# Moving half of a residual's gate rows behind a down projection, and five small loads to another DMA queue

## The chip, the core and the metric

The kernel runs on one core of a Trainium2 chip. The metric is the device time of one execution in microseconds; each time given is a median of several executions. In the profile PE is the matrix engine (TensorE), PEld its weight loads, DVE the vector engine, ACT the scalar engine, POOL GpSimd, and SP the engine whose queue issues most DMAs. An engine's name with a q behind it (ACTq, SPq) is its sequencer, which issues DMAs and waits.

## What is computed

A trunk of two layers over 512 tokens of width 1024, batch 1, in float32. Cut to what matters:

```python
for i in range(2):
    sh1, sc1, g1, sh2, sc2, g2 = split(silu(c) @ ada_w[i] + ada_b[i], 6)
    h = x * (1 + sc1) + sh1
    y = neighbourhood_mixer(h) if i == 0 else gqa_mixer(h)      # gqa: RMS-normed q, k with gains, rotary tables cos, sin
    x = layer_norm(ALPHA * x + (1 + g1) * y, ln_g[i, 0], ln_b[i, 0])
    h = x * (1 + sc2) + sh2
    y = hierarchical_moe(h)                                     # 32 experts, top 2: (silu(h Wg) * (h Wu)) Wd, weighted
    x = layer_norm(ALPHA * x + (1 + g2) * y, ln_g[i, 1], ln_b[i, 1])
```

The layer norm in front of the mixture leaves its gain and bias out at first; they are applied when x is needed again, as `x * ALPHA * ln_g + ALPHA * ln_b`. This is the step called `residual` below.

## The kernel before

Tokens lie in four tiles `X[0..3]` of 128 x 1024. Each layer is a mixer, its output projection and a router, and then the mixture of experts. Each expert takes up to 64 tokens, and two experts make a pair that fills 128 partitions. The 32 experts are 16 pairs, which the function `moe` goes through in 8 rounds `q` of two pairs, `a` and `b`. A round is, in the order of the code and of PE (whose order is written by hand here): `gate_up(a)` (products `gu` of the gathered tokens `xT` with 8 weight tiles of 1 MB), `turn` (four transposes), some filling work, `down(a)` (products `pd` of the transposed `hx` with 4 weight tiles of 1 MB), `gate_up(b)`, the gathering of the next round's tokens (products `gc` with the one-hot `OH`), and `down(b)`. In rounds 1 to 7 the filling work around `down(a)` adds the previous round's results to `X` (`combine`, also into tiles named `gc`).

In round 0 there is nothing to combine yet. There the filling work is `gate2` (the rows 1 + g2), `counts` (tokens per expert) and `residual(0)` and `residual(1)`, one for each half of 512 columns. Each of them spreads two rows of the modulation table over 128 partitions by a matmul, `pg` (gain) and `pb` (bias), into PSUM tiles named `gc`, of which there are two, and DVE then works through the four tiles of `X` with four pairs of instructions (lines 1367 and 1368):

```python
pg = pp.tile([P, F], F32, name="gc", bufs=2)
self.row(pg, l, 12 + h)
pb = pp.tile([P, F], F32, name="gc", bufs=2)
self.row(pb, l, 14 + h)
for t in range(NT):
    nc.vector.scalar_tensor_tensor(x, x, ALPHA, pg, op0=OP.mult, op1=OP.mult)
    nc.vector.scalar_tensor_tensor(x, pb, ALPHA, x, op0=OP.mult, op1=OP.add)
```

`self.row` is one matmul of 512 columns (two records in the trace). `down` writes the half x into `pd0` or `pd1`, and DVE (line 1413) and ACT (line 1414) and DVE again (line 1415) turn it into `YH` and `YL`.

All weights come through one queue, SP's, in a fixed order (`plan`), into a ring of buffers: the function `W` issues the next loads whenever buffers are free, and SP waits in its order for the PE instructions that read the buffer last. DVE, ACT and POOL are ordered by a scheduler.

`mixer1`, the second layer's mixer, begins with loads of the rotary tables (`rt`, from `in_rope`, one DMA) and of four rows of 64 norm weights (`gn`, tiles named `kk`, from `in_gain`, four DMAs, each spread over 128 partitions). POOL multiplies them (line 730) into the tables that the keys and queries use later. Beside that ACT and POOL or DVE split the first weights `w` (keys and values) into a high part `wh` (ACT, line 312) and a low part `wl` (line 313), PE transposes X into tiles `pt`, ACT makes `hTH` of it (line 419), and PE multiplies it with `wh` and `wl` into tiles `pj`.

Of the kernel before, what the change touches and what calls it, by code (L numbers as in the profile page):

```python
# [17 lines left out]
P = 128  # L18
# [5 lines left out]
HD = 64  # L24
# [37 lines left out]
def bcast(ap, shape):  # L62
    return ap.to_broadcast(shape)


class Trunk:
# [651 lines left out]
    def mixer1(self, st, qS):  # L718
        nc, a, tc = self.nc, self.a, self.tc
# [2 lines left out]
        V = qv.tile([P, NT, 256], F32, name="V")  # L722
        with tc.tile_pool(reuse_waits="tile", name="m1", bufs=1) as pool, tc.tile_pool(reuse_waits="tile", name="m1p", bufs=2, space=PSUM) as pp:
            rt = pool.tile([P, 4, NT, HD], F32, name="rt")
            nc.scalar.dma_start(rt[:, 0:2], a["rope"])
            gn = pool.tile([P, 4, HD], F32, name="kk", bufs=6)
            for i in range(4):
                nc.scalar.dma_start(gn[:, i, :], bcast(a["gain"][i:i + 1], [P, HD]))
            for i in (2, 3, 0, 1):
                nc.gpsimd.tensor_tensor(rt[:, i], rt[:, i % 2], bcast(gn[:, i:i + 1, :], [P, NT, HD]), op=OP.mult)  # L730
            hH = pool.tile([P, KD, S], F32R, name="hTH")
# [547 lines left out]
    def moe(self, l, zH, zL, G2, rt, OH):  # L1279
        nc, X, tc = self.nc, self.X, self.tc  # L1280
        NQ = E // 4
        with tc.tile_pool(reuse_waits="tile", name=f"mo{l}", bufs=2) as pool, \
# [35 lines left out]
            def gather(q, kk):  # L1318
                if kk == 0:
                    xT[q] = pool.tile([P, KD, 256], F32, name="xT", bufs=1)  # L1320
                ps = pp.tile([P, 2, 256], F32, name="gc", bufs=2)
                for k2 in range(2):
                    k = 2 * kk + k2
                    for t in range(NT):
                        for x, hh in ((0, zH), (1, zL)):
                            self.mm(ps[:, k2, :], hh[t][:, 128 * k:128 * k + 128], oh[:, t, :],
                                    t == 0 and x == 0, t == NT - 1 and x == 1)
                for k2 in range(2):
                    scaled(q, 2 * kk + k2, ps[:, k2, :])
# [20 lines left out]
            def combine(js, t, h):  # L1350
                c = slice(512 * h, 512 * h + 512)
                ps = pp.tile([P, F], F32, name="gc", bufs=2)
                n = 0
                for j in js:
                    for y in (YH, YL):
                        self.mm(ps, OT[j][:, t, :], y[j][:, c], n == 0, n == 2 * len(js) - 1)
                        n += 1
                nc.vector.tensor_tensor(X[t][:, c], X[t][:, c], ps, op=OP.add)  # L1358

            def residual(h):  # L1360
# [5 lines that stand above are left out]
                    x = X[t][:, 512 * h:512 * h + 512]  # L1366
                    nc.vector.scalar_tensor_tensor(x, x, ALPHA, pg, op0=OP.mult, op1=OP.mult)
                    nc.vector.scalar_tensor_tensor(x, pb, ALPHA, x, op0=OP.mult, op1=OP.add)

            def gate2(h):  # L1370
                ps = pp.tile([P, F], F32, name="tp", bufs=2)
                self.row(ps, l, 10 + h)
                nc.vector.tensor_scalar(G2[:, 512 * h:512 * h + 512], ps, 1.0, None, op0=OP.add)

            def gate_up(j):
                q, o = j // 2, 128 * (j % 2)
                gu = []
                for n in range(2):
                    g = pp.tile([P, F], F32, name=f"gu{n}")
                    gu.append(g)  # L1380
                    for kh in range(2):
                        w = [self.W(("gu", l, 2 * j + i, n, kh)).rearrange("p (k n) -> p k n", k=4) for i in range(2)]
                        for k in range(4):
                            kk = 4 * kh + k
                            for i in range(2):
                                self.mm(g[64 * i:64 * i + 64], xT[q][:, kk, o + 64 * i:o + 64 * i + 64], w[i][:, k, :],
                                        kk == 0, kk == KD - 1)
                    if n == 0:
                        h = pool.tile([P, F], F32, name="h", bufs=1)
                        nc.scalar.activation(h, gu[0], AF.Silu)  # L1390
                nc.vector.tensor_tensor(h, h, gu[1], op=OP.mult)  # L1391
                return h

            def turn(h):
                pt = pp.tile([P, 4, P], F32, name="tp", bufs=2)
                for f in range(4):
                    self.tr(pt[:, f, :], h[:, 128 * f:128 * f + 128])
                hx = pool.tile([P, F], F32, name="hx", bufs=1).rearrange("p (f s) -> p f s", f=4)
                nc.scalar.activation(hx, pt, AF.Copy)
                return hx  # L1400

            def down(j, hx):
                YH[j] = pool.tile([P, D], F32R, name="YH", bufs=2)
                YL[j] = pool.tile([P, D], F32R, name="YL", bufs=2)
                for x in range(2):
                    pd = pp.tile([P, F], F32, name=f"pd{x}")
                    w = [self.W(("dn", l, 2 * j + i, x)).rearrange("p (k n) -> p k n", k=4) for i in range(2)]
                    for f in range(4):
                        for i in range(2):
                            self.mm(pd[64 * i:64 * i + 64], hx[:, f, 64 * i:64 * i + 64], w[i][:, f, :], f == 0, f == 3)  # L1410
                    c = slice(512 * x, 512 * x + 512)
                    y = pool.tile([P, F], F32, name=("h", "hx")[x], bufs=1)
                    nc.vector.scalar_tensor_tensor(y, pd, GS[j][:, 2:3], G2[:, c], op0=OP.mult, op1=OP.mult)  # L1413
                    nc.scalar.activation(YH[j][:, c], y, AF.Copy)  # L1414
                    nc.vector.tensor_tensor(YL[j][:, c], y, YH[j][:, c].bitcast(F32), op=OP.subtract)
# [3 lines left out]
            def seed(ns):  # L1419
                for n in ns:  # L1420
                    h, t = units[n]
                    tag = ("gc", "gc", "gu0", "tp", "gu1", "tp", "pd0", "pd1")[n]
                    acc[h, t] = pp.tile([P, F], F32, name=tag, bufs=2 if n in (0, 1, 3, 5) else 1)
                    if n < NSEED[1]:
                        self.mm(acc[h, t], self.ident, X[t][:, 512 * h:512 * h + 512], True, False)
# [24 lines left out]
            for q in range(NQ):  # L1450
                a, b = 2 * q, 2 * q + 1
                h = gate_up(a)
                if q == 0:
                    fill = [lambda: gate2(0), lambda: gate2(1), lambda: self.counts(pool, pp, rt),
                            lambda: residual(0), lambda: residual(1)]
                else:
                    fill = [lambda t=t, x=x: combine((a - 2, a - 1), t, x) for t, x in th]
                for f in fill[:2]:
                    f()
                hx = turn(h)  # L1460
                for f in fill[2:]:
                    f()
                down(a, hx)
                if q + 1 < NQ:
                    self.mark(OH, rt, q + 1, 0, NT)
                else:
                    XR = [self.take() for _ in range(2)]
                    rt["XR"] = [XR[t // 2][:, D * (t % 2):D * (t % 2) + D] for t in range(NT)]
                h = gate_up(b)
                if q + 1 < NQ:  # L1470
                    gather(q + 1, 0)
                    hx = turn(h)
                    gather(q + 1, 1)
                    for n in range(2):
                        slots(a + 2, n)
                        gather(q + 1, 2 + n)
                    for n in range(2):
                        slots(b + 2, n)
                else:
                    self.act_table("natural_log_exp_and_others")  # L1480
                    for t, x in th[:2]:
                        combine((a,), t, x)
                    hx = turn(h)
                    for t, x in th[2:]:
                        combine((a,), t, x)
                    if l == DEPTH - 1:
                        rt["out"] = self.rows(l, pool.tile([P, KD, 256], F32, name="xT", bufs=1), pp, "gc", 2)
                    seed(range(NSEED[0]))
                down(b, hx)
# [146 lines left out]
```

## Time and profile before

| | |
|---|---|
| time, median of 3 executions | 1670.0 us (1669.55 to 1672.5) |
| the profiled execution | 1673.29 us, span of its instructions 1671.6 us |
| busy share of the span | PE 94%, PEld 54%, DVE 42%, ACT 26%, POOL 10% |
| mean granted PE clock | 0.972 of full speed |
| DMA | 493.17 MB, mean 295 GB/s |

The page cuts the span into 40 slices and tells for each how busy the engines were, which clock PE was granted and what the DMA engines moved. The timeline lists instructions in order of time, with the idle time before them and what ended it. The chain of waits is followed back from the last instruction. The windows give busy time by stretch.

### The profile page before, as it was taken

How to read it: one execution, taken by the hardware profiler on the slowest of the kernel's cores; microseconds unless marked ns; L12 is line 12 of the kernel's file. 1: busy time of each engine (PE TensorE's matmuls, PEld its weight loads, DVE VectorE, ACT ScalarE, POOL GpSimd, SP SyncE). 2: the span in 40 equal slices, each digit the busy share in tenths (PEclk: the TensorE clock that was granted, in tenths of full speed). 3: DMA queues.
4: the chain of work that ended last, by engine and by line, in shares of the span. 5: the costliest groups of instructions: out<-in, count | busy, mean ns of one | idle time of the engine just before them, and what ended most of it. 6: DMA issues, size and time to landing. Idle time of an engine off the chain costs nothing. (4 is left out here: it accounts for less than half of the span.)

```text
span 1671.6 us, 21362 instructions
## 1 busy us (share of the span) xinstructions
PE 1574.7 (94%) x8490; PEld 906.6 (54%) x8490; DVE 700.6 (42%) x1605; ACT 437.6 (26%) x934; POOL 162.3 (10%) x99
## 2 busy tenths in 40 slices
PE   7899997989999999999979989998999999999995
PEld 4676664773544545455448866766354545545442
DVE  3434545574232322323256865666432232323235
ACT  2343335231110111111134475453011111101112
POOL 2322212010000000000014250011000000000001
PEclk9999997999999999999989989999999999999997
DMA  9587872357999999999932000035899999999981
GB/s 328 196 309 269 331 306 104 137 202 295 417 419 420 419 419 420 419 419 420 420 125 102 26 1 25 1 125 206 368 416 420 420 420 420 419 420 420 419 332 51
DMA packets 76198, 493.17 MB, mean 295 GB/s; under 512 B 9876, under 2 KB 11284, under 8 KB 18876
## 3 DMA queue, kind: packets, MB, share of 16 engines
q1 hardware_dynamic: 71916, 485.05, 71.4%
q10 hardware_dynamic: 4176, 6.69, 1.2%
q8 instruction: 69, 1.13, 0.3%
q14 instruction: 37, 0.30, 0.1%
HBM read 489.61 MB, written 2.10 MB: 294 GB/s over the span
## 5 line engine op out<-in xcount | busy, mean ns | idle before, releaser
L300 PE MATMUL gu<-w,xT 128*64 128x512 f32 x2048 | 445.0, 592 | 0.0
L300 PEld LDWEIGHTS gu<-w,xT 128*64 128x64 f32 x2048 | 146.8, 137 | 291.6 <-issue 287.0
L300 PE MATMUL pd<-w,hx 128*64 128x512 f32 x1024 | 228.0, 598 | 0.0
L1391 DVE TENSOR_TENSOR h<-h,gu 128x512 f32<-128x512 f32 x32 | 22.0, 688 | 370.4 <-PE gu L300 370.4
L300 PEld LDWEIGHTS pd<-w,hx 128*64 128x64 f32 x1024 | 70.9, 137 | 140.3 <-issue 136.7
L300 PE MATMUL gc<-OH,zH 128*128 128x256 f32 x480 | 121.5, 291 | 2.6 <-DVE OH L1276 2.6
L300 PE MATMUL gc<-OH,zL 128*128 128x256 f32 x480 | 118.6, 284 | 0.0
L300 PE MATMUL gc<-YH,OT 128*128 128x512 f32 x244 | 104.2, 427 | 1.0 <-DVE X L1358 1.0
L1358 DVE TENSOR_TENSOR X<-X,gc 128x512 f32<-128x512 f32 x128 | 87.4, 688 | 39.3 <-PE gc L300 39.3
L300 PEld LDWEIGHTS gc<-OH,zH 128*128 128x128 f32 x480 | 92.5, 193 | 14.9 <-issue 11.4
L300 PE MATMUL gc<-YL,OT 128*128 128x512 f32 x244 | 96.3, 394 | 0.0
L300 PEld LDWEIGHTS gc<-OH,zL 128*128 128x128 f32 x480 | 92.6, 193 | 0.0
L300 PE MATMUL pw<-w,oH 128*128 128x512 f32 x256 | 86.3, 408 | 0.0
L1414 ACT ACTIVATE YH<-h 128x512 fp32r<-128x512 f32 x32 | 20.2, 630 | 233.6 <-DVE h L1413 233.6
L300 PE MATMUL pj<-wh,hTH 128*128 128x256 f32 (+1 forms) x272 | 71.2, 304 | 9.1 <-ACT hTH L419 4.0
L1294 ACT ACTIVATE xT<-gc,A 128x256 f32<-128x256 f32 x60 | 33.8, 566 | 173.9 <-PE gc L300 173.9
L300 PE MATMUL pj<-wl,hTH 128*128 128x256 f32 (+1 forms) x272 | 68.0, 292 | 0.0
L300 PE MATMUL pj<-wh,hTL 128*128 128x256 f32 (+1 forms) x272 | 65.6, 293 | 0.8 <-DVE hTL L427 0.8
L300 PEld LDWEIGHTS gc<-YH,OT 128*128 128x128 f32 x244 | 45.8, 188 | 37.3 <-DVE X L1358 15.8
L1292 DVE TENSOR_SCALAR xT<-gc,A 128x256 f32<-128x256 f32 x60 | 32.5, 545 | 76.9 <-ACT xT L1294 76.5
L1390 ACT ACTIVATE h<-gu 128x512 f32<-128x512 f32 x32 | 19.1, 597 | 173.0 <-PE gu L300 173.0
L303 PE MATMUL pt<-c_ident,pr 128*128 128x128 f32 x384 | 59.5, 283 | 2.1 <-ACT pr L862 2.0
(345 smaller groups left out, 2355.9 us busy)
## 6 DMA issues: line engine op xcount, KB each, us to landing
w<-in_gu SPq DMA_DIRECT2D x256, 1024.0 KB, 14.3
w<-in_dn SPq DMA_DIRECT2D x128, 1024.0 KB, 13.5
w<-in_ada SPq DMA_DIRECT2D x40, 1024.0 KB, 7.9
wq<-in_wqk SPq DMA_DIRECT2D x16, 512.0 KB, 3.6
w<-in_wo SPq DMA_DIRECT2D x8, 1024.0 KB, 5.8
w<-in_adaq SPq DMA_DIRECT2D x6, 1024.0 KB, 12.0
bias<-in_nab ACTq DMA_DIRECT2D x24, 256.0 KB, 3.4
w<-in_wq SPq DMA_DIRECT2D x4, 1024.0 KB, 4.9
```

Source lines behind the costliest of these rows:

```text
L300: return self.nc.tensor.matmul(out, l, r, start=start, stop=stop, **kw)
L303: self.nc.tensor.transpose(out, in_, self.ident)
L1292: nc.vector.tensor_scalar(xT[q][:, k, :], ps, s, b, op0=OP.mult, op1=OP.add)
L1294: nc.scalar.activation(xT[q][:, k, :], ps, AF.Identity, scale=s, bias=b)
L1358: nc.vector.tensor_tensor(X[t][:, c], X[t][:, c], ps, op=OP.add)
L1390: nc.scalar.activation(h, gu[0], AF.Silu)
L1391: nc.vector.tensor_tensor(h, h, gu[1], op=OP.mult)
L1414: nc.scalar.activation(YH[j][:, c], y, AF.Copy)
```

## The change

Two edits. In `moe`, round 0 no longer does `residual(1)` in front of `down(a)`, but right behind it. In `mixer1`, the five small loads are issued by SP's queue instead of ACT's.

```diff
@@ mixer1
             rt = pool.tile([P, 4, NT, HD], F32, name="rt")
-            nc.scalar.dma_start(rt[:, 0:2], a["rope"])
+            nc.sync.dma_start(rt[:, 0:2], a["rope"])
             gn = pool.tile([P, 4, HD], F32, name="kk", bufs=6)
             for i in range(4):
-                nc.scalar.dma_start(gn[:, i, :], bcast(a["gain"][i:i + 1], [P, HD]))
+                nc.sync.dma_start(gn[:, i, :], bcast(a["gain"][i:i + 1], [P, HD]))
@@ moe
                 if q == 0:
-                    fill = [lambda: gate2(0), lambda: gate2(1), lambda: self.counts(pool, pp, rt),
-                            lambda: residual(0), lambda: residual(1)]
+                    fill = [lambda: gate2(0), lambda: gate2(1), lambda: self.counts(pool, pp, rt), lambda: residual(0)]
                 else:
                     fill = [lambda t=t, x=x: combine((a - 2, a - 1), t, x) for t, x in th]
...
                 for f in fill[2:]:
                     f()
                 down(a, hx)
+                if q == 0:
+                    residual(1)
```

In the first layer, PE's rows between the counting product and `down(a)` were these (`mod` is the modulation table, `c_indc` picks a row of it):

```order
L300 LDWEIGHTS ones
L300 MATMUL tp<-Mb,ones 128x32
L300 MATMUL gc<-mod_67,c_indc 128x512 x4
L300 MATMUL pd_3298<-w_3178,hx 64x512
L300 MATMUL pd_3298<-w_3180,hx 64x512
```

Now two of the four row products stand there, and the end of `down(a)` with the start of `gate_up(b)` (`gu`) reads so:

```order
L300 MATMUL pd_3303<-w_3182,hx 64x512
L300 MATMUL pd_3303<-w_3184,hx 64x512
L300 MATMUL gc<-mod_67,c_indc 128x512 x2
L300 MATMUL gu_3333<-w_3186,xT 64x512
L300 MATMUL gu_3333<-w_3188,xT 64x512
```

The two products of `residual(1)` have moved behind the 16 of `down(a)`. The second layer has the same difference.

On DVE, in the first layer, behind the last instruction of `residual(0)` (the first row; X_63 to X_66 are the four tiles of X, L1158 to L1162 belong to `counts`):

```order
 L1368 SCALAR_TENSOR_TENSOR X_66<-gc,X_66 128x512
+L1413 SCALAR_TENSOR_TENSOR h<-pd_3286,GS,G_3009 128x512
+L1415 TENSOR_TENSOR YL<-h,YH 128x512
+L1158 TENSOR_SCALAR hx<-cntx 128x32 x7
+L1159 TENSOR_REDUCE nbx<-hx 128x32
 L1367 SCALAR_TENSOR_TENSOR X_63<-X_63,gc 128x512
+L1161 TENSOR_REDUCE hx<-nbx 128x1
 L1367 SCALAR_TENSOR_TENSOR X_64<-X_64,gc 128x512
+L1162 CAST tot<-hx 128x1
 L1368 SCALAR_TENSOR_TENSOR X_63<-gc,X_63 128x512
+L1413 SCALAR_TENSOR_TENSOR hx<-pd_3303,GS,G_3009 128x512
 L1368 SCALAR_TENSOR_TENSOR X_64<-gc,X_64 128x512
```

The first half of `down(a)` and the counts are now worked off ahead of the eight instructions of `residual(1)`, and the second half in the midst of them.

At the start of `mixer1`, ACT's rows (the first two are the end of the branch that closes the first layer):

```order
 L1169 UNCONDITIONAL_BRANCH x2
-L725 DMA rt<-in_rope 128x512
-L728 DMA kk<-in_gain 128x64 x4
 L312 ACTIVATE wh<-w_5752 128x1024 x2
 L419 ACTIVATE hTH<-pt,c_6307 128x512 x2
```

and SP's, where the loads now stand ahead of the fourth load of query weights:

```order
 L1169 UNCONDITIONAL_BRANCH x2
+L725 DMA rt<-in_rope 128x512
+L728 DMA kk<-in_gain 128x64 x4
 L272 DMA w_6311<-in_wq 128x2048
 L272 DMA w_6534<-in_wo 128x2048
```

ACT now goes from the branch straight to the split of the weights. PE's scheduler also puts two transposes of this stage some 25 products later than before.

## Rows read from the trace of the kernel before

**Rows 1.** Page: GB/s moved by DMA in 40 equal slices of the span.

```profile
GB/s 328 196 309 269 331 306 104 137 202 295 417 419 420 419 419 420 419 419 420 420 125 102 26 1 25 1 125 206 368 416 420 420 420 420 419 420 420 419 332 51
```

**Rows 2.** Timeline of PE, first layer, round 0: start, duration, instruction, idle before.

```profile
393.50 1.96 PE L300 MATMUL gc<-mod,c_indc 128*128 128x512 f32 x4
398.45 3.78 PE L300 MATMUL gc<-mod,c_indc 128*128 128x512 f32 x4 [2.99 <-DVE X L1367]
402.16 8.27 PE L300 MATMUL pd<-w,hx 128*64 128x512 f32 x32
410.27 13.90 PE L300 MATMUL gu<-w,xT 128*64 128x512 f32 x64
```

**Rows 3.** Timeline of DVE, same stretch.

```profile
394.72 1.28 DVE L1367 SCALAR_TENSOR_TENSOR X<-X,gc 128x512 f32<-128x512 f32 x2 [0.84 <-PE gc L300]
...
398.31 1.28 DVE L1368 SCALAR_TENSOR_TENSOR X<-gc,X 128x512 f32<-128x512 f32 x2
...
407.08 0.75 DVE L1413 SCALAR_TENSOR_TENSOR h<-pd,GS,G 128x512 f32<-128x512 f32 x1 [1.13 <-PE pd L300]
...
410.51 0.71 DVE L1158 TENSOR_SCALAR hx<-cntx 128x32 f32<-128x32 f32 x7 [1.29 <-PE pd L300]
```

**Rows 4.** Timeline of PE, second layer, round 0.

```profile
1181.13 1.96 PE L300 MATMUL gc<-mod,c_indc 128*128 128x512 f32 x4
1186.09 3.67 PE L300 MATMUL gc<-mod,c_indc 128*128 128x512 f32 x4 [2.99 <-DVE X L1367]
1189.68 7.09 PE L300 MATMUL pd<-w,hx 128*64 128x512 f32 x32
1196.60 13.90 PE L300 MATMUL gu<-w,xT 128*64 128x512 f32 x64
```

**Rows 5.** Chain of waits in order of time: start, duration, what.

```profile
906.17 0.86 PE pg L300 x2
...
1226.74 13.73 PE gu L300 x64
...
1285.77 13.73 PE gu L300 x64
```

**Rows 6.** Windows: busy time of each engine; last PEclk, DMA share, GB/s.

```profile
403.00:408.00 5.00, 5.00 (x22) 1.60 (x20) 3.70 (x6) 0.14 (x1) 0.00 (x0) 0.84 0.00 0
1191.00:1194.00 3.00, 3.00 (x16) 1.00 (x14) 3.00 (x6) 0.00 (x0) 0.00 (x0) 1.00 0.00 0
```

**Rows 7.** Timeline of SP, near the first layer's end.

```profile
807.16 0.33 SPq L272 DMA_DIRECT2D w<-in_gu  x1
```

**Rows 8.** DMA issues of 807 to 808 us: count, size, us to landing.

```profile
w<-in_gu SPq DMA_DIRECT2D x1, 1024.0 KB, 20.5
```

**Rows 9.** Timeline of PE, the first layer's last `gate_up`.

```profile
823.57 13.90 PE L300 MATMUL gu<-w,xT 128*64 128x512 f32 x64
```

**Rows 10.** Timeline of ACT at the start of `mixer1`.

```profile
867.88 0.34 ACTq L725 DMA_DIRECT2D rt<-in_rope  x1
868.33 1.81 ACTq L728 DMA_DIRECT2D kk<-in_gain  x4
870.19 2.00 ACT L312 ACTIVATE wh<-w 128x1024 fp32r<-128x1024 f32 x2 [2.48 <-DMA rt<-in_rope]
...
881.12 0.78 ACT L419 ACTIVATE hTH<-pt,c 128x512 fp32r<-128x512 f32 x1 [2.84 <-PE pt L303]
```

**Rows 11.** Timeline of PE at the start of `mixer1`.

```profile
867.85 1.94 PE L303 MATMUL pt<-c_ident,X 128*128 128x128 f32 x8 [6.23 <-ACTq L1169]
872.91 0.58 PE L300 MATMUL pj<-wh,hTH 128*128 128x256 f32 x1 [3.12 <-ACT hTH L419]
```

**Rows 12.** Windows of the same stage, as in rows 6.

```profile
875.00:879.00 4.00, 4.00 (x20) 4.00 (x20) 1.60 (x2) 2.54 (x4) 4.00 (x4) 0.50 0.10 16
879.00:885.00 6.00, 4.93 (x40) 4.46 (x39) 2.18 (x2) 3.88 (x6) 4.64 (x2) 1.00 0.58 183
```

**Rows 13.** Timeline of SP around the start of `mixer1`.

```profile
834.08 44.11 SPq L272 DMA_DIRECT2D w<-in_wq  x4
```

## The prediction

> **What bounds the kernel now.** I read the page first, then the windows, then the timelines of the three places that the change touches, PE and its partner engine side by side. PE is busy for 94% of the span, so a saving counts only where PE stands still or where PE's own work gets less, and only if the weights keep up.
>
> Two long stretches of the page, the expert stages of the two layers, move 416 to 420 GB/s all the time [rows 1]. The reader is to see two things running flat out together there. One round of two pairs takes PE 1285.77 - 1226.74 = 59.03 us [rows 5], and it eats 24 tiles of 1 MB (8 + 4 for each pair), 25.17 million bytes, which at 419.5 GB/s take 60.0 us. So the stream is a little slower than PE, loses about 1 us on it in each round, and lives on the lead that it has when the stage begins. What is left of the lead at the end decides whether PE may become faster. Near the first layer's end a tile was issued at 807.16 and landed 20.5 us later, at 827.7 [rows 7, 8]. It is one of the fourth pair of tiles of the gate_up that starts at 823.57 and lasts 13.90 [rows 9], so it is needed at 823.57 + 3/4 x 13.9 = 834.0. It lay there for 6.3 us. PE, not the stream, sets the pace up to the end.
>
> In round 0 the reader is to see PE standing still. The first half's row products start at 393.50, and the next ones only at 398.45, because both PSUM tiles are held until DVE has worked through X [rows 2, 3]. DVE takes 394.72 to 398.31 for three double rows, that is 0.60 us for each of its eight instructions. down follows only at 402.16. PE's clock has meanwhile fallen to its lower level (1.2 of 2.4 GHz; 0.84 of the full one over 403 to 408 [rows 6]), and the four products of the second half, which take 1.72 us at full clock (two records in 0.86 [rows 5]), take 3.7. The second layer shows the same [rows 4].
>
> At the start of mixer1, PE has 8 transposes from 867.85 on, and then waits 3.12 us for ACT [rows 11]. ACT issues five DMAs from 867.88 to 868.33 + 1.81 = 870.14, and its first split starts at 870.19 [rows 10]. The view puts that wait down to the landing of the rotary table. But the split reads neither table, and it starts 0.05 us behind the last issue: ACT was its own hindrance.
>
> **The change, part by part.** *residual(1) behind down, first layer.* Nothing of the arithmetic goes away. down can now start right behind the first half's products, at 393.50 + 1.72 = 395.22, since hx and the weights are long there. At full clock down takes 1196.60 - 1189.68 = 6.92 us [rows 4]. The moved products add 1.72. gate_up(b) starts at 395.22 + 6.92 + 1.72 = 403.86 instead of 410.27 [rows 2]: **6.4 us**. Of this, 1.2 us are the slow clock in down itself (410.27 - 402.16 - 6.92). If the clock fell all the same, 5.2 would be left; I take the whole, since PE's long idle time is gone.
>
> *Second layer.* By the same sum 1181.13 + 1.72 + 6.92 + 1.72 = 1191.49 instead of 1196.60 [rows 4]: **5.1 us**.
>
> What hides the eight DVE instructions: they ran in PE's way and now run beside gate_up(b), 13.73 us [rows 5]. At down's end, at 402.1, DVE is free (residual(0) is done at 399.6, the first evacuation at 0.75 + an ACT step + 0.75 some 2 us later [rows 3]). What it then has is 0.71 + three small reductions (under 0.75 together) + 8 x 0.60 + 2 x 0.75 = 7.8 us, and the next that PE needs of it is the product h, 1.72 + 13.73 = 15.4 us after down's end. There are 7 us to spare. The moved products' PSUM tiles are released by residual(0)'s reads at 399.6, 2.5 us before PE comes to them. Nothing else is late next on these engines.
>
> *Does the stream follow?* In both layers it stood with all buffers full, while PE stalled: no byte moves from 403 to 408 and from 1191 to 1194 [rows 6]. down frees those buffers 6.9 us earlier now, and the stream goes on without that gap. So it gains about what PE gains, at least 5 and 3 us. Even if it gained nothing in the first layer, a lead of 6.3 against 6.4 would lose 0.1 us.
>
> *Five DMAs on SP.* ACT saves their issue: its split can start at 867.88 instead of 870.19, **2.3 us** [rows 10]. PE's transposes end at 869.79, the two splits (2.00) at 869.9, so the whole chain of ACT, hTH and PE moves by the same 2.3. The loads cost SP as much, but SP's next load, the fourth of query weights, left only at the end of a row that lasts to 834.08 + 44.11 = 878.2, because its buffer is read until then [rows 13]; so SP has time. The places that the loads write were free by 867.88 at the latest, when ACT's first issue went out, so POOL's tables come no later than before either. Bounds: 0, if the row's reading is right and the landing was what ACT waited for, and 2.3. I take 2.3, as the 0.05 us speak for it. The rule of the Trainium skill (DMA: Bandwidth & Descriptors, section Issuing engines are not separate DMA queues) is that another issuing engine saves only the sequencer's time for starting a DMA, which is usually small beside the transfer. By "usually small" this term would be about 0 and the sum 11.5; the row says 2.3 us of ACT's own time, on the path, for five small DMAs.
>
> *Clock in mixer1.* PE runs at half clock (0.50, so 1.2 GHz) there until 879, and at the full one behind it [rows 12], so its 6.1 us of products from 872.91 on [rows 11] would be 3.0 us at full clock, and ACT waits 2.84 us for them at 881.12 [rows 10]. With the gap of 3.12 us behind the transposes shrunk to 0.8, the clock may rise earlier in PE's work: at most 3.0 us more. It may also rise later; I let that cost 1.5 us, half of the spread of the runs shown. Nearest is the row of before, so I take **0.5 us**.
>
> PE's two transposes that the scheduler moved cost nothing: PE does the same rows without a gap in that stretch (4.00 of 4.00 us busy [rows 12]).
>
> Sum: 6.4 + 5.1 + 2.3 + 0.5 = 14.3 us. The profiled execution took 1673.3 us, 3.3 above the median of 1670.0 and 1.7 above its span. All terms are differences inside it, so they are taken from the median: **1655.7 us**.
>
> **The rivals.** *The ACT edit does nothing on the path.* For it: the view's own releaser. Against it: the 0.05 us. Time: 1670.0 - 11.5 = 1658.5.
>
> *The stream takes the gain back.* If the weights set the pace of the expert stage, PE would wait for them before its end, and only the second edit would count: 1670.0 - 2.8 = 1667.2. For it: 60.0 us against 59.03 in each round. Against it: 6.3 us of lead at the end, and the gap in the stream that closes. The Trainium skill (DMA: Bandwidth & Descriptors, section Specifications) gives about 358 GB/s as one core's share of the HBM. By that the stream would be behind PE from the start and this rival would hold. The rows show 416 to 420 [rows 1].
>
> *Slower: the clock.* gate_up(b) now comes right behind the moved products. Should PE get only half clock in it, 13.73 us become 27.5 in each layer: 1670.0 - 14.3 + 27.5 = 1683. It decides from 28 us of additional half clock on. For it: the clock did fall just ahead of this place before [rows 6]. Against it: only after 3 us in which PE did nothing, and that idle time goes.
>
> **How the numbers follow.** The forecast 0.78, the ACT edit without effect 0.14, the stream 0.05, the clock 0.03. The forecast's own bounds are 1670.0 - 11.5 - 2.3 - 3.0 = 1653.2 and 1670.0 - (11.5 - 1.2) - 2.3 + 1.5 = 1658.9. With the first rival and the scatter of a median the range is 1653.0 to 1660.0. A measurement of this kernel tells about 0.2% (3.3 us) from no change. The first two cases are faster by more (0.92), the stream's 2.8 us count as the same (0.05), and the clock's case is slower (0.03).
>
> **What would show it.** Right: in both layers down starts some 1.8 us behind the first row products, PE has no wait on line 1367, the two moved products lie between pd and gu, and gate_up(b) starts 10.4 us behind the first row products (393.50 to 403.9). DVE has the second evacuation done before gate_up(b) ends, and DMA has no empty stretch in round 0. In mixer1, ACT's first split follows its last normalisation at once, and PE's wait behind the 8 transposes is under 1 us. Wrong: waits of PE on w<-in_gu or w<-in_dn late in a layer, a new wait of ACT's first split on another DMA, POOL's tables holding up the low parts of the weights, or half clock inside gate_up.

## The result and the profile after

The changed kernel took 1659.12 us (median of 5 executions, 1656.66 to 1660.54), beside it the kernel before 1671.91 (5 executions, 1669.55 to 1674.84). The ratio is 0.9925, with a 95% interval of 0.9910 to 0.9941: 12.5 us less, between 9.9 and 15.0. The profiled execution took 1659.12 us, its span is 1657.4 (1671.6 before).

The timeline of PE in the first layer's round 0 (start, duration, instruction) now reads:

```profile
393.49 1.96 PE L300 MATMUL gc<-mod,c_indc 128*128 128x512 f32 x4
395.38 7.09 PE L300 MATMUL pd<-w,hx 128*64 128x512 f32 x32
402.40 1.98 PE L300 MATMUL gc<-mod,c_indc 128*128 128x512 f32 x4
404.31 13.95 PE L300 MATMUL gu<-w,xT 128*64 128x512 f32 x64
```

Against [rows 2], the wait for line 1367 is gone, `down` runs at full clock, and `gate_up(b)` starts 10.82 us behind the first row product instead of 16.77. The second layer, same view, is the same to 0.01 us, where [rows 4] had 15.47:

```profile
1171.56 1.96 PE L300 MATMUL gc<-mod,c_indc 128*128 128x512 f32 x4
1173.45 7.09 PE L300 MATMUL pd<-w,hx 128*64 128x512 f32 x32
1180.47 1.98 PE L300 MATMUL gc<-mod,c_indc 128*128 128x512 f32 x4
1182.38 13.95 PE L300 MATMUL gu<-w,xT 128*64 128x512 f32 x64
```

DVE works off the first half of `down` at once, and the last of its eight moved instructions in the first layer is done at 410, 8 us before `gate_up(b)` ends at 418.2 (timeline of DVE):

```profile
399.50 0.74 DVE L1413 SCALAR_TENSOR_TENSOR h<-pd,GS,G 128x512 f32<-128x512 f32 x1
...
409.30 0.69 DVE L1368 SCALAR_TENSOR_TENSOR X<-gc,X 128x512 f32<-128x512 f32 x1
418.41 0.69 DVE L1391 TENSOR_TENSOR h<-h,gu 128x512 f32<-128x512 f32 x1 [8.41 <-PE gu L300]
```

The windows of both places (busy time of each engine; the last three columns are PE's clock, DMA share and GB/s) show the stream without its gap [rows 6], and PE at full clock:

```profile
403.00:408.00 5.00, 5.00 (x22) 1.66 (x22) 4.97 (x14) 0.63 (x1) 0.00 (x0) 1.00 1.01 418
1180.00:1192.00 12.00, 12.00 (x54) 4.02 (x52) 7.37 (x20) 1.23 (x2) 0.00 (x0) 1.00 1.02 422
```

At the start of `mixer1`, the timelines of SP, ACT and PE:

```profile
855.94 0.34 SPq L725 DMA_DIRECT2D rt<-in_rope  x1
861.95 1.75 SPq L728 DMA_DIRECT2D kk<-in_gain  x4
```

```profile
859.65 2.23 ACT L1542 ACTIVATE X<-w,rsx 128x512 f32<-128x512 f32 x3 [1.11 <-DVE rsx L1092]
862.04 2.00 ACT L312 ACTIVATE wh<-w 128x1024 fp32r<-128x1024 f32 x2 [0.17 <-ACTq L1169]
```

```profile
862.02 1.94 PE L303 MATMUL pt<-c_ident,X 128*128 128x128 f32 x8 [6.25 <-ACTq L1169]
864.77 0.58 PE L300 MATMUL pj<-wh,hTH 128*128 128x256 f32 x1 [0.81 <-ACT hTH L419]
```

ACT's split follows its last normalisation (done at 861.88) 0.16 us later, and PE waits 0.81 us behind its transposes instead of 3.12 [rows 11].

To see where all the time went I cut each profiled execution at PE instructions that every kernel has: the start of the first layer's first `gate_up` (front), from the end of a round-0 `gate_up(a)` to the start of `gate_up(b)` (round 0 of either layer), from there to the layer's last `gate_up` (experts), from the first of `mixer1`'s transposes to its first product `pj` (issue), from there to the last `pj`, and from the last `pj` to the second layer's first `gate_up` (rest of mixer). All values but the span are differences of starts in us. The stages left out agree to 0.4 us, apart from two: in e7 it is 45.13 us instead of some 44.3 from the last `gate_up` to the transposes, and in e1 and e2 the second layer's first `gate_up` takes 15.0 and 15.1 us instead of 13.9.

| kernel | front | round 0, first | experts, first | issue | pj | rest of mixer | round 0, second | span |
|---|---|---|---|---|---|---|---|---|
| before | 376.75 | 19.63 | 413.30 | 5.06 | 94.88 | 196.59 | 18.33 | 1671.6 |
| changed | 376.74 | 13.69 | 413.42 | 2.75 | 94.89 | 195.15 | 13.69 | 1657.4 |
| changed, again (e11) | 373.92 | 13.69 | 413.39 | 2.75 | 95.41 | 195.38 | 13.69 | 1655.4 |
| rows only (e1) | 371.95 | 13.69 | 413.41 | 5.07 | 94.96 | 194.35 | 13.69 | 1655.3 |
| rows only, again (e12) | 376.42 | 13.69 | 413.43 | 5.07 | 95.04 | 196.65 | 13.69 | 1661.1 |
| loads only (e2) | 372.96 | 16.99 | 413.37 | 2.75 | 95.41 | 196.07 | 18.34 | 1664.1 |
| table on ACT (e3) | 374.40 | 13.69 | 413.40 | 3.13 | 95.28 | 195.67 | 13.69 | 1656.3 |
| other PSUM (e4) | 375.66 | 13.39 | 413.34 | 2.75 | 95.34 | 195.19 | 13.39 | 1656.1 |
| both behind (e5) | 374.86 | 20.96 | 413.85 | 2.75 | 94.70 | 195.14 | 20.96 | 1670.5 |
| two buffers fewer (e6) | 372.71 | 13.69 | 413.38 | 2.69 | 95.71 | 195.62 | 13.69 | 1654.6 |
| four buffers fewer (e7) | 374.00 | 13.69 | 415.80 | 2.70 | 94.78 | 194.11 | 13.69 | 1656.7 |
| 17 issues on ACT (e9) | 374.42 | 13.69 | 413.38 | 12.83 | 94.48 | 196.77 | 13.69 | 1666.0 |
| warm PE (e8) | 373.56 | 13.69 | 413.39 | 2.43 | 94.15 | 197.33 | 13.69 | 1655.7 |
| other PSUM, warm (e10) | 370.88 | 13.39 | 413.36 | 2.42 | 95.69 | 194.90 | 13.39 | 1651.4 |

From before to the changed kernel 5.94 us come from round 0 of the first layer, 4.64 from that of the second, 2.31 from the issue, and 1.44 from the rest of the mixer, less 0.2 in the two expert stages: 14.2, the difference of the spans. The fourth can't be put down to the change: the same code gave 194.35 in e1 and 196.65 in e12. Over all kernels the rest of the mixer varies from 194.1 to 197.3 and the front, where they don't differ, from 370.9 to 376.8. A single span is therefore worth less than its stages.

### The profile page after: what moved, and what is told of

It is laid out like the page before. It is cut to its first block, busy times and chain, and to the rows that moved or that the text cites. A ratio compares the mean times of both kernels' runs of the same rounds, so it can differ in the third digit from the quotient of the medians.

```text
span 1657.4 us, 21364 instructions
## 1 busy us (share of the span) xinstructions
PE 1569.4 (95%) x8490; PEld 903.9 (55%) x8490; DVE 700.5 (42%) x1605; ACT 437.8 (26%) x934; POOL 162.7 (10%) x99
## 5 line engine op out<-in xcount | busy, mean ns | idle before, releaser
L313 POOL TENSOR_TENSOR wl<-w,wh 128x1024 fp32r<-128x1024 f32 x19 | 46.1, 2431 | 559.5 <-DMA kk<-in_gain 494.4
L300 PEld LDWEIGHTS gc<-OH,zH 128*128 128x128 f32 x480 | 92.7, 193 | 14.7 <-issue 11.4
## 6 DMA issues: line engine op xcount, KB each, us to landing
w<-in_gu SPq DMA_DIRECT2D x256, 1024.0 KB, 13.9
w<-in_adaq SPq DMA_DIRECT2D x6, 1024.0 KB, 11.5
```

Source lines behind the costliest of these rows:

```text
L300: return self.nc.tensor.matmul(out, l, r, start=start, stop=stop, **kw)
L313: (eng or nc.gpsimd).tensor_tensor(lo, src, h.bitcast(F32), op=OP.subtract)
```

## The experiments

**Each edit alone (e1, e2).** e1 is the changed kernel with the five loads back on ACT's queue. e2 has the loads on SP's queue and before's order in round 0.

```diff
 e1
-            nc.sync.dma_start(rt[:, 0:2], a["rope"])
+            nc.scalar.dma_start(rt[:, 0:2], a["rope"])
...
-                nc.sync.dma_start(gn[:, i, :], bcast(a["gain"][i:i + 1], [P, HD]))
+                nc.scalar.dma_start(gn[:, i, :], bcast(a["gain"][i:i + 1], [P, HD]))
 e2
-                    fill = [..., lambda: residual(0)]
+                    fill = [..., lambda: residual(0), lambda: residual(1)]
...
-                if q == 0:
-                    residual(1)
```

> Only the move of the second half's row products; the five loads stay on ACT's queue. The theory (two independent savings, the rows worth 6.0 and 4.7 us in the two layers): about 10.6 us under before, 1661 us at a before of 1672, some 2 to 4 us above the changed kernel; the layer 0 part of the trace as in the changed kernel (gate_up(b) about 10.8 us behind the first row product), and in mixer1 ACT's first split again about 2.3 us behind the branch with PE waiting about 3.1 us for hTH. The rival that the loads gave nothing: the same time as the changed kernel, within 1 us.

> Only the five loads on SP's queue; both halves' row products stay in front of down. The theory: 2.3 us of ACT's time at the start of mixer1 and up to 1.4 us more from the clock behind it, so 2.3 to 3.7 us under before, about 1669 us at a before of 1672; PE waits 3 us for DVE in round 0 of both layers as in before; PE's wait for hTH at mixer1's start under 1 us. The rival that the landing of the rotary table was what ACT waited for and the time went elsewhere: 0 us, and ACT's first split still late.

e1 took 1658.02 us, ratio to before 0.9937 (0.9922 to 0.9953), e2 1666.01 us, 0.9989 (0.9978 to 1.0001). Most of the gain is the rows'. By these times alone the loads could be worth nothing: e1's interval holds the changed kernel's 0.9925, and e2's holds 1. The stages say why. In e1 the issue stage is 5.07 us, as before, but its front happened to be 4.8 us shorter than that of the changed kernel's execution. In e2 that stage is 2.75, and the rest is before's. e2 also shows what round 0 costs when the clock stays up (timeline of PE):

```profile
389.71 1.96 PE L300 MATMUL gc<-mod,c_indc 128*128 128x512 f32 x4
394.66 2.32 PE L300 MATMUL gc<-mod,c_indc 128*128 128x512 f32 x4 [2.98 <-DVE X L1367]
396.91 7.09 PE L300 MATMUL pd<-w,hx 128*64 128x512 f32 x32
403.83 13.90 PE L300 MATMUL gu<-w,xT 128*64 128x512 f32 x64
```

The wait is the same as in [rows 2], but the second pair of row products takes 2.32 us and not 3.78, and `down` 7.09 and not 8.27. The granted clock is 1.00 over 394 to 397, where before has 0.50 over 398 to 402. `gate_up(b)` starts 14.12 us behind the first row product, 3.30 more than in the changed kernel, and not 5.95.

**The loads once more (e11, e12).** The changed kernel and e1's code side by side on one chip.

> The changed kernel itself, once more, on the same chip as the next three, so that they can be set against it: 1657 to 1660 us.

> The rows' move alone, once more, beside the changed kernel on one chip. The five loads are all that lies between the two. By the theory of the traces (PE's first product 5.07 instead of 2.75 us behind the start of its transposes) the median is 2.3 us above the changed kernel; by the rival that this is given back later, 0 to 1 us.

The changed kernel took 1657.05 us, 0.9929 (0.9912 to 0.9945), the rows alone 1660.91, 0.9949 (0.9930 to 0.9968). This time the loads are worth 3.9 us by the medians, but the intervals overlap. Over both comparisons the rows alone stand at 0.9943 and the changed kernel at 0.9927: 0.16%, 2.7 us, which fits the 2.3 of the stages and e2's 0.11%, 1.8 us. Times alone would not have settled it.

**What ACT waited for (e3, e9).** In e3 only the rotary table goes back to ACT's queue. In e9 all loads do, and each of the four for the norm weights is cut in four pieces of 16 columns.

```diff
 e3
-            nc.sync.dma_start(rt[:, 0:2], a["rope"])
+            nc.scalar.dma_start(rt[:, 0:2], a["rope"])
 e9, beside that
-                nc.sync.dma_start(gn[:, i, :], bcast(a["gain"][i:i + 1], [P, HD]))
+                for j in range(0, HD, 16):
+                    nc.scalar.dma_start(gn[:, i, j:j + 16], bcast(a["gain"][i:i + 1, j:j + 16], [P, 16]))
```

> The changed kernel with one of the five loads back on ACT's queue, the rotary table, and the four loads of norm weights left on SP's. This tells what ACT's first split waited for in before. If it was the engine's own time for issuing (one issue of about 0.4 us instead of five of 2.3): the split starts about 0.4 us later than in the changed kernel and the time is within 0.5 us of it. If it was the landing of the rotary table, as the view of before has it: the split starts about 2.3 us later, PE waits about 3.1 us for hTH again, and the time is 2.3 us or more above the changed kernel.

> The changed kernel with the loads back on ACT's queue and each of the four norm-weight loads cut in four of 16 columns: 17 issues instead of before's five, the same bytes. If ACT's own time for issuing is the price: some 0.45 us each, 7.6 us in all, ACT's first split 7.6 us behind the branch, PE's first product about 8 us behind the end of its transposes and its start behind them 10.4 us (2.75 in the changed kernel, 5.06 in before), and the whole 5 to 8 us above the changed kernel. If the landing of the table was the price: as before, 2.3 us above the changed kernel.

e3 took 1658.04 us, 0.9933 (0.9917 to 0.9949). Its timeline of ACT:

```profile
859.67 0.34 ACTq L725 DMA_DIRECT2D rt<-in_rope  x1
860.06 2.00 ACT L312 ACTIVATE wh<-w 128x1024 fp32r<-128x1024 f32 x2 [0.55 <-ACTq L1169]
```

The table was issued on ACT and the split began 0.05 us behind the issue. The trace has no landing for the table, but none of the much smaller norm-weight loads (32 KB each, for 256) landed sooner than 2.8 us after its issue. So the split didn't wait for the table to land, and the releaser that [rows 10] names is wrong. e9's timeline of ACT, and behind it that of PE:

```profile
859.66 0.34 ACTq L725 DMA_DIRECT2D rt<-in_rope  x1
860.11 9.59 ACTq L729 DMA_DIRECT2D kk<-in_gain  x16
869.75 2.00 ACT L312 ACTIVATE wh<-w 128x1024 fp32r<-128x1024 f32 x2 [10.26 <-DMA kk<-in_gain]
```

```profile
872.47 0.58 PE L300 MATMUL pj<-wh,hTH 128*128 128x256 f32 x1 [10.89 <-ACT hTH L419]
```

The split starts 0.05 us behind the last of 17 issues, and the issue stage grows by 10.08 us against the changed kernel. An issue of 16 columns took 0.60 us, not the 0.45 that I had assumed, hence 12.83 and not 10.4. The whole took 1663.82 us, 0.9957 (0.9943 to 0.9970), which is about 5 us above the changed kernel by the ratios to before (0.9957 against 0.9925 and 0.9929). The profiled execution, the longest of the five (1667.74), has all 10 us in its span. That the other four (1663.05 to 1664.04) show only about half of the 10 is not explained: they have no trace, and the fronts alone differ by up to 5.9 us from execution to execution.

**Whether the stall was the two PSUM tiles (e4, e5).** In e4 PE's order is before's, but the second half's row products go to the tiles `gu0` and `gu1`, which are free there. In e5 the first half moves behind `down` as well.

```diff
 e4
-                pg = pp.tile([P, F], F32, name="gc", bufs=2)
+                pg, pb = [pp.tile([P, F], F32, name=f"gu{n}") if h else pp.tile([P, F], F32, name="gc", bufs=2) for n in range(2)]
...
-                pb = pp.tile([P, F], F32, name="gc", bufs=2)
 and round 0 as in e2
 e5
-                    fill = [lambda: gate2(0), lambda: gate2(1), lambda: self.counts(pool, pp, rt), lambda: residual(0)]
+                    fill = [lambda: gate2(0), lambda: gate2(1), lambda: self.counts(pool, pp, rt)]
...
                 if q == 0:
+                    residual(0)
                     residual(1)
```

> Before's order of products on PE (both halves in front of down), with the loads on SP's queue, and the second half's two row products written to the two PSUM tiles gu0 and gu1 instead of waiting for the two named gc. If the stall of round 0 was nothing but the wait for those two PSUM tiles: PE runs the four row products in one piece, down starts about 3.8 us behind the first of them, and gate_up(b) starts as early as in the changed kernel, or up to 1.5 us later where it must wait for DVE to have read gu0 and gu1; the whole within 0 to 3 us of the changed kernel. If the place in the order matters by itself (DVE's eight instructions in front of down's evacuation hold PE up anyway): about 10 us slower than the changed kernel, near the kernel with only the loads moved.

> The changed kernel with the first half's row products also moved behind down(a), so that all four row products stand in one piece between down(a) and gate_up(b). If what the change removed is the wait for two PSUM tiles with nothing of PE's behind it, the wait is back at the new place: PE starts down at once, then does two row products, waits some 3 us for DVE's line 1367, does the other two, and gate_up(b) starts 3.0 to 5 us later than in the changed kernel, in both layers: 6 to 10 us above it, about 1666. The rival that any place behind down is as good: the same time as the changed kernel.

e4 took 1657.02 us, 0.9927 (0.9912 to 0.9942), no different from the changed kernel. PE's timeline there:

```profile
392.41 1.96 PE L300 MATMUL gc<-mod,c_indc 128*128 128x512 f32 x4
394.21 1.88 PE L300 MATMUL gu<-mod,c_indc 128*128 128x512 f32 x4
396.02 7.09 PE L300 MATMUL pd<-w,hx 128*64 128x512 f32 x32
402.94 13.90 PE L300 MATMUL gu<-w,xT 128*64 128x512 f32 x64
```

All four row products stand in one piece, in before's order, without a wait. So the place in the order does not matter by itself; the wait for the two tiles does. e5 took 1672.15 us, 1.0017 (1.0006 to 1.0028): slower than before, although it moves more of the work out of `down`'s way and has the loads' gain.

```profile
391.99 7.09 PE L300 MATMUL pd<-w,hx 128*64 128x512 f32 x32 [0.23 <-ACT hx L1399]
399.01 1.98 PE L300 MATMUL gc<-mod,c_indc 128*128 128x512 f32 x4
405.99 3.78 PE L300 MATMUL gc<-mod,c_indc 128*128 128x512 f32 x4 [5.00 <-DVE X L1367]
409.70 14.41 PE L300 MATMUL gu<-w,xT 128*64 128x512 f32 x64
```

The wait is back behind `down`, as expected, but it is 5.00 us and not 3, since DVE has the second of `down`'s evacuations to do in the midst of line 1367's and 1368's instructions (line 1413 at 402.21, line 1415 at 404.06). The clock falls again too (3.78 us). In both layers round 0 takes 20.96 us, 14.5 in all above the changed kernel, where I had expected 6 to 10.

**Whether the weights follow (e6, e7).** The first layer's expert stage loses two, and four, of its weight buffers of 1 MB.

```diff
 e6
-NWY = (3, 1)
+NWY = (1, 1)
 e7, beside that
-                self.free += [no] * 2
```

> The changed kernel with two weight buffers of 1 MB fewer in the first layer's expert stage. A weight tile takes 2.5 us of the stream, so the lead at the last gate_up of that layer should shrink from about 6.9 to about 1.9 us. If PE and not the stream sets the pace there, the time from round 0's gate_up(b) to the last gate_up stays at 413.4 us and the whole is that of the changed kernel within 1 us. If the stream sets the pace: 2 to 5 us longer.

> The changed kernel with four weight buffers of 1 MB fewer in the first layer's expert stage. The lead would shrink from 6.9 by 10.0 us to -3.1, so here the stream must become the bound near the stage's end: the time from round 0's gate_up(b) to the last gate_up grows from 413.4 to about 416.5 us, with waits of PE on weight loads, and the whole is about 3 us above the changed kernel. If the lead is no measure of it: no wait on weights, and the same time; if the stream already hung by the buffers: 10 us more.

e6 took 1656.00 us, 0.9916 (0.9900 to 0.9931). The fourth pair of tiles of the last `gate_up` had its second load issued at 802.04; it landed 20.0 us later, at 822.0, and was needed at 813.66 + 3/4 x 13.9 = 824.1. The lead was 2.0 us, and PE lost nothing: 413.38 us for the stage. e7 took 1658.69 us, 0.9932 (0.9916 to 0.9947), its timeline of PE, and a window of the stage's end:

```profile
756.72 14.74 PE L300 MATMUL gu<-w,xT 128*64 128x512 f32 x64
...
817.36 14.76 PE L300 MATMUL gu<-w,xT 128*64 128x512 f32 x64
```

```profile
757.00:815.00 58.00, 58.00 (x294) 28.64 (x292) 15.40 (x31) 7.57 (x16) 0.00 (x0) 1.00 1.01 420
```

Four of the last five `gate_up`s take 14.7 to 14.8 us instead of 13.90, at full clock (1.00), since each now waits inside for its tiles. In the last one the second load of the fourth pair was issued at 814.54 and landed 13.9 us later, at 828.4, where it was due at 817.36 + 3/4 x 13.9 = 827.8. The view shows no wait there, only longer rows. The stage grew by 2.4 us, and the next up to the transposes by 0.85 (45.13 for 44.28), 3.2 in all, where the lead's balance said 3.1. On the same chip e7 was 2.7 us above e6, which fits; against the changed kernel on other chips (1659.12 and 1657.05) it doesn't show, as fronts differ by more. The stream ran at 420 GB/s over that window. The Trainium skill (DMA: Bandwidth & Descriptors, section Specifications) gives about 358 GB/s as a core's limit to the HBM; by that figure the stream would have been the bound with all buffers. The measurement differs and decides: the stream becomes the bound only with four of them gone.

**The clock at the start of `mixer1` (e8, e10).** In e8 PE does six products without use in the wait ahead of the transposes; their sum times zero is added to a norm weight. e10 has this and e4's tiles.

```diff
 e8
+            if l == 0:
+                warm = pp.tile([P, F], F32, name="gc", bufs=2)
+                for n in range(6):
+                    self.mm(warm, self.ident, zH[0][:, 0:F].bitcast(F32), n == 0, n == 5)
+                self.warm = self.cst.tile([P, 1], F32, name="warm")
+                nc.vector.tensor_scalar(self.warm, warm[:, 0:1], 0.0, None, op0=OP.mult)
             self.scales(pool, rt, 0, NT)
...
+            nc.vector.tensor_scalar(gn[:, 0, :], gn[:, 0, :], self.warm, None, op0=OP.add)
             for i in (2, 3, 0, 1):
```

> The changed kernel with six added products of 512 columns (about 5.2 us of PE) at the end of the first layer, where PE stands idle for 6.25 us in front of mixer1's transposes; their sum is multiplied by zero and added to a norm weight, so nothing else changes. This tests the clock's part at mixer1's start (0.50 of full speed there). If PE's idle time is what takes the clock down: full clock over the transposes and the first products, PE's transposes 1 us and the next 6 us of products 3 us shorter, ACT's wait of 2.14 us for them gone, and the whole 2 to 4 us under the changed kernel. If the clock does not depend on that idle stretch: the same time; if the added products are in the way: up to 1 us slower.

> The version that should be the fastest: the second half's row products in tiles gu0 and gu1 in front of down (round 0 took 27.28 instead of 27.57 us with them), the loads on SP's queue, and the six added products of the kernel e8. Against the changed kernel: 0.6 us for round 0 in both layers and 2 to 4 us if the added products hold the clock up, so 1654 to 1657 us; if they do nothing, 1658.

e8 took 1656.64 us, 0.9924 (0.9906 to 0.9942), e10 1655.90, 0.9923 (0.9903 to 0.9943); the changed kernel beside them 1657.05, 0.9929. PE's timeline in e8, and below it the first 6 us of `mixer1` as windows of the changed kernel and of e8:

```profile
852.39 5.31 PE L300 MATMUL gc<-zH,c_ident 128*128 128x512 f32 x12
859.13 1.06 PE L303 MATMUL pt<-c_ident,X 128*128 128x128 f32 x8 [1.43 <-DVEq L1170]
861.56 0.39 PE L300 MATMUL pj<-wh,hTH 128*128 128x256 f32 x1 [1.37 <-ACT hTH L419]
```

```profile
862.00:868.00 6.00, 5.17 (x23) 4.79 (x24) 5.00 (x10) 5.22 (x7) 3.74 (x3) 0.50 0.19 36
```

```profile
859.00:865.00 6.00, 3.82 (x28) 3.24 (x28) 5.28 (x11) 6.00 (x8) 3.95 (x3) 1.00 0.31 79
```

The added products do hold the clock at its full level (2.4 GHz), 1.00 instead of 0.50, and PE's transposes take 1.06 us instead of 1.94. But nothing of 2 to 4 us follows: ACT is busy for all 6.00 us now, PE waits for it longer (1.37 for 0.81), and the transposes start 0.3 us later. From the transposes to the last `pj` it takes 2.43 + 94.15 = 96.6 us against 97.6 and 98.2 in the changed kernel, and 98.1 in e10. About 1 us may be had there, but no time shows it. e4's tiles are worth 0.30 us in each round 0, and none of these versions can be told from the changed kernel.

## Why the prediction was right, and where its sizes were off

*The rows' move.* Its mechanism held in every step that the prediction named: no wait on line 1367, the two products between `pd` and `gu`, no gap in the stream, DVE done in time. e4 shows the cause by another way, with the old order and other tiles. The start of `gate_up(b)` came 10.82 us behind the first row product, not 10.36. The 0.46 us lie where one kind of product follows another: `down` starts 1.89 us behind the row products and not 1.72, they start 7.02 behind it and not 6.92, `gate_up(b)` 1.91 behind them and not 1.72.

The term that was mis-sized is the first layer's 6.4, of which the prediction said "I take the whole, since PE's long idle time is gone". It took one execution's half clock for a part of the kernel, and it counted too little of that time as the clock's: 1.2 us, those in `down`. e2's first round 0, with the clock up, is 2.65 us shorter than before's, 1.19 of it in `down` and 1.46 in the second pair of row products. The four round 0 with the stall, in before and e2, took 19.63, 18.33, 16.99 and 18.34 us; without it, every one took 13.69. So a layer gives 3.30 to 5.94 us, 4.6 on the mean, and both together 9.3 instead of 11.5. With the issue's 2.3 that makes 11.6; the two comparisons gave 12.5 and 11.8, where the forecast was 14.3.

*The five loads.* 2.3 us were predicted, 2.31 are in the stage, and e3 and e9 show that it was ACT's own time for issuing: one issue costs 0.38 us there (3.13 for 2.75), five 2.3, seventeen 10.1. From the transposes to the last `pj` it takes 99.9 to 100.1 us with the loads on ACT (before, e1, e12) and 97.6 to 98.2 without (changed, e11, e2), so the 2 us last at least to there. The first rival falls. What the Trainium skill says (DMA: Bandwidth & Descriptors, section Issuing engines are not separate DMA queues), that another issuer saves just the sequencer's time, agrees with this. That this time is usually small does not help here, where the engine that issues is the one PE waits for.

*The clock in `mixer1`.* I had 0.5 us. The clock did rise earlier, between 869 and 870, some 7.3 us behind the start of the transposes, where before has the half clock until 879 [rows 12], 11.2 us behind it. Windows of the changed kernel:

```profile
865.00:870.00 5.00, 5.00 (x27) 5.00 (x28) 4.03 (x4) 4.26 (x6) 4.84 (x5) 0.57 0.48 156
870.00:875.00 5.00, 4.33 (x36) 3.85 (x34) 1.36 (x2) 2.86 (x6) 5.00 (x3) 1.00 0.15 62
```

But no gain shows: from the first `pj` to the last it takes 94.88 us in before and 94.89 and 95.41 in the two runs of the changed kernel. The 1.44 us in the rest of the mixer lie behind the projections and within that stage's scatter. The bound of 3.0 us was too wide: with the clock held up in e8, at most some 1 us is found.

*The stream.* It did not take the gain back. e6 shows that the lead could have shrunk by 5 us more without loss, and e7 that this lead is the right measure.

*Slower by half clock in `gate_up(b)`.* It did not happen: `gate_up(b)` takes 13.95 us in both layers, and the window from 403 to 408 has 1.00.

The time came out 1.4 to 3.4 us above the predicted, inside the range, and that in part by luck. The forecast's own bounds ended at 1658.9, and 1659.12 is inside only because the range was widened for the first rival and for scatter; before, taken as 1670.0, measured 1671.91 beside it.

## What to carry to other kernels

When PE waits for PSUM tiles that a slow reader holds, either other tiles or independent products put between the two uses remove the wait, the products only if they fill the whole time that the reader needs: moving both halves together brought the wait back, and longer. Small loads belong on the queue of an engine that has nothing due then; count their issue time as work of that engine. Where stages that the change does not touch scatter by several us, compare the stage from trace to trace, and take a stall's price from more than one execution when a fallen clock is part of it.

## What was not expected of the hardware

Cutting a load in pieces made each issue longer: 0.45 us for one of the four of 64 columns (1.81 for four [rows 10]), and 0.60 for one of 16 columns (9.59 for sixteen in e9). The half clock falls at other moments from execution to execution: in round 0 of the first layer with the stall, the same two row products took 3.78 us in before and 2.32 in e2, whose code is the same up to there, and twice (e1 and e2, second layer) `gate_up(a)` took some 15 us instead of 13.9 (granted clock 0.60 over 1150 to 1155 in e1). A PE that waits for weights inside a run of products shows no idle time in the timeline, only a longer row (14.76 us for 13.90 in e7).
